# Five chunks instead of three in the last group of mixer 0's output projection, two of seven combinations transposed beside the first FFN pairs

## The chip, the cores and the metric

One core of a Trainium2 chip runs the whole program. The metric is device microseconds of one execution; times of several runs and one profiled execution are given. TensorE (PE) multiplies and transposes, VectorE (DVE), ScalarE (ACT) and GpSimd (POOL) work beside it, and SyncE (SP) issues nearly all transfers. Each engine takes its instructions in a fixed order.

## The reference, cut to what matters

A two-layer decoder trunk on x of 1024 tokens by 1024 channels, float32. Layer 0 has a mixer with two head groups, whose outputs are concatenated (2048 channels) and projected; layer 1 has attention. After each mixer and each FFN comes a LayerNorm of the residual sum:

```python
mix = jnp.concatenate([y_a, y_b], axis=-1) @ w_out
x = layer_norm(ALPHA * x + mix, ln_mix_g, ln_mix_b)
h = causal_dwconv(x @ w_up, conv_w, conv_b)
u, g = jnp.split(h, [D_FF], axis=-1)
x = layer_norm(ALPHA * x + (u * silu(g)) @ w_down, ln_ffn_g, ln_ffn_b)
```

## The kernel before, in words

**Matrix products in float32.** Each operand is split into a rounded high part (a cast on ScalarE, line 116) and a remainder (a subtraction on VectorE, line 117). A product is three matmuls of 128 x 128 by 128 x 512: high by high, high by low, low by high.

**The output projection** (end of `mixer0`, from line 731) runs over 16 chunks of 128 channels in four groups, g = 0 to 3, of 5, 4, 4 and 3 chunks: 0 to 4, 8 to 11, 12 to 15, 5 to 7. Chunks 0 to 7 are y_a, read back from `ya_d`; 8 to 15 are y_b, from `u_d`. `operands` loads a chunk of y and of the weight and splits both into places that the table `places` names: X(n) and E(n) are tiles of two pools, `weights()` and `raws` tiles of the weights' pool, `centre` the two tiles of x.T. For each group `down` takes the 8 token blocks in turn: six matmuls per chunk into one of three PSUM tiles, then `evac` adds the sum to the residual row r[i] on VectorE. In the last group it also runs the LayerNorm and writes r[i] to `x_d`. `late=1` there means that the first three blocks take all chunks but one, and then the last chunk, block by block. The blocks' order is 0, 4, 1, 5, 2, 6, 3, 7.

**The seam.** The FFN's up projection (`ffn_pairs`) multiplies seven combinations of x.T instead of eight quarters: blocks i and i + 4 of r give the corners, halves are added and subtracted on VectorE in `combine` (lines 195 to 209), and each result is transposed by TensorE in runs of four into one of two PSUM banks and split by ScalarE and VectorE (`to_xc`). There are 28 such runs: two for each of blocks 0 to 3, five for each of 4 to 7. They are queued as closures that `down`, and after it `ffn_pairs`, call.

**Pairs.** For j of 0 to 21, pair j holds chunk j of u and of g. `pair_begin` makes two products, x and y, with combinations 0 and 1; `pair_end` makes five, into the banks of x, z and v:

```python
self.multiply(z, w["s1"], 3)
nc.scalar.copy(c[:, 3, :], z)
self.multiply(v, w["s3"], 5)
V.tensor_add(c[:, 3, :], c[:, 3, :], v)
self.multiply(z, w["s4"], 2, more=True)
self.multiply(x, w["s2"], 4, more=True)
nc.scalar.copy(c[:, 1:3, :], x.unsqueeze(1).broadcast_to([P, 2, 512]))
V.tensor_add(c[:, 3, :], c[:, 3, :], x)
self.multiply(v, w["a22"], 6, more=True)
V.tensor_add(c[:, 1:3, :], c[:, 1:3, :], zv.rearrange("p (a b) -> p a b", a=2))
```

GpSimd forms sums of the weights (lines 222 to 225, tile ws) from the loaded chunks (wr); both are split into tiles wo, a ring of ten places. `gate` runs the convolution (ScalarE line 165, four taps on VectorE, line 167), silu and the product u*g. A scheduler orders each engine's instructions when the program is built, so the code's order is only a priority.

Of the kernel before, what the change touches and what calls it, by code (L numbers as in the profile page):

```python
# [10 lines left out]
F32 = mybir.dt.float32  # L11
F32R = mybir.dt.float32r
BF16 = mybir.dt.bfloat16
AF = mybir.ActivationFunctionType
ALU = mybir.AluOpType
# [3 lines left out]
P = 128  # L19
L = 1024  # L20
# [5 lines left out]
NFF = DFF // P  # L26
# [4 lines left out]
XLAG = 2  # L31
# [4 lines left out]
class Ring:  # L36


    def __init__(self, places):
        self.places, self.n = list(places), -1  # L40
# [6 lines left out]
class Net:  # L47
# [11 lines left out]
    def __init__(self, ctx, tc, io):  # L59
        self.ctx, self.tc, self.nc, self.io = ctx, tc, tc.nc, io  # L60
        pool = lambda name, **k: ctx.enter_context(tc.tile_pool(name=name, **k))
        self.const = pool("const", bufs=1)
        self.xp = pool("xT", bufs=1)
        self.wp = pool("w", bufs=1)
        self.ps = pool("ps", bufs=1, space=PSUM)
        self.mm_next, self.after = 0, []
        self.low_engine = self.nc.vector
        self.dr = pool("dr", bufs=1, space=DRAM)
        self.small = pool("small", bufs=4)
        self.consts()  # L70
# [48 lines left out]
    def raw(self, src):  # L119
        t = self.wp.tile([P, D], F32, tag="wraw", name="wraw", bufs=2)  # L120
        self.nc.sync.dma_start(t, src)
        return t
# [69 lines left out]
        h, l = self.xc[m]  # L192
        self.split(h[:, :, ts], l[:, :, ts], ps.rearrange("p (k t) -> p k t", k=4))

    def combine(self, i, r, engine):

        a, b = r[i], r[i + 4]
        lo, hi = slice(0, 512), slice(512, D)
        minus = lambda out, x, y: engine.tensor_tensor(out, x, y, op=ALU.subtract)
        self.to_xc(2, i, b[:, hi])  # L200
        minus(a[:, lo], b[:, lo], a[:, lo])
        self.to_xc(3, i, a[:, lo])
        minus(b[:, lo], b[:, hi], b[:, lo])
        self.to_xc(5, i, b[:, lo])
        minus(a[:, hi], a[:, hi], b[:, hi])
        minus(b[:, hi], b[:, hi], a[:, lo])
        self.to_xc(4, i, b[:, hi])
        engine.tensor_tensor(a[:, hi], a[:, hi], a[:, lo], op=ALU.add)
        self.to_xc(6, i, a[:, hi])

    def pair_a(self, a, ops):

# [46 lines left out]
    def pair_end(self, w, c, x):  # L259
        nc, V = self.nc, self.nc.vector  # L260
        zv = self.mm_ps()
        z, v = zv[:, :512], zv[:, 512:]
        self.multiply(z, w["s1"], 3)
        nc.scalar.copy(c[:, 3, :], z)
        self.multiply(v, w["s3"], 5)
        V.tensor_add(c[:, 3, :], c[:, 3, :], v)  # L266
        self.multiply(z, w["s4"], 2, more=True)
        self.multiply(x, w["s2"], 4, more=True)
        nc.scalar.copy(c[:, 1:3, :], x.unsqueeze(1).broadcast_to([P, 2, 512]))  # L269
        V.tensor_add(c[:, 3, :], c[:, 3, :], x)  # L270
        self.multiply(v, w["a22"], 6, more=True)
        V.tensor_add(c[:, 1:3, :], c[:, 1:3, :], zv.rearrange("p (a b) -> p a b", a=2))  # L272

# [143 lines left out]
    def ffn_pairs(self, layer):  # L417


        nc, tc, io = self.nc, self.tc, self.io  # L420
        V = nc.vector
        y_d = self.dr.tile([NFF, P, L], F32, name="y_d")
        first = [self.rp.tile([P, L], F32, tag=f"r{i}", name="wr") for i in (0, 4, 2)]
        rt = lambda i: self.rp.tile([P, L], F32R, tag=f"r{i}", name="wo")
        ops = Ring([rt(1), rt(5), *self.two(self.eb, 3, "wo", F32R), rt(6), rt(3), rt(7)])
        sums = Ring(self.two(self.eb, 2, "ws"))
        cs = Ring([self.big(self.eb, n, "c").rearrange("p k l -> p (k l)").rearrange("p (a b) -> p a b", a=4)
                   for n in range(2)])
# [2 lines left out]
        raws = Ring(wide["wraw"] + wide["wh"][:1])  # L431
        ug = Ring(wide["wh"][1:] + wide["wl"])

        def raw(c, t=None):
            t = raws() if t is None else t
            nc.sync.dma_start(t, io["ffn_w_up"][layer, c])
            return t
# [7 lines left out]
            V.tensor_mul(u, u, g)  # L445
            nc.sync.dma_start(y_d[j], u)

        a = [raw(j, t) for j, t in enumerate(first[:2])]
        w = [self.pair_a(t, ops) for t in a]
        c = [cs(), cs()]  # L450
        while len(self.after) > 1:
            self.after.pop(0)()
        x = [self.pair_begin(w[0], c[0])]
        self.after.pop(0)()
        then = self.pair_b(w[0], a[0], raw(NFF, first[2]), ops, sums)
        next(then)
        ops.places += [rt(2), rt(0), rt(4)]
        next(then, None)
        x.append(self.pair_begin(w[1], c[1]))
        then = self.pair_b(w[1], a[1], raw(NFF + 1), ops, sums)  # L460
        next(then)
        for j in range(NFF):
            if 2 <= j + 1 < NFF:
                a, b = raw(j + 1), raw(NFF + j + 1)
                w.append(self.pair_a(a, ops))
                then = self.pair_b(w[j + 1], a, b, ops, sums)
# [10 lines left out]
        staged = Ring(staged)  # L477
# [14 lines left out]
        for n, places in enumerate(groups):  # L492
            begins, final = n == 0, n == len(groups) - 1
            ys, ws = [], []
            for place in places():
                for into, src in ((ys, y_d[done]), (ws, io["ffn_w_down"][layer, done])):
                    raw = staged()
# [5 lines left out]
            if begins:  # L503
                staged.places.append(last)
                r = [self.rp.tile([P, D], F32, tag=f"r{i}", name=f"r{i}") for i in range(NT)]
# [21 lines left out]
    def mixer0(self):  # L527
        nc, tc, io = self.nc, self.tc, self.io
        V = nc.vector
# [3 lines left out]
        first = []  # L533
        for k in range(KD):
            if k < 2:
                first.append(self.weight(win[32 + k]))
            raw = self.rp.tile([P, L], F32, tag=f"r{k}", name="xraw")
# [10 lines left out]
        if True:  # L548
            xs = [self.rp.tile([P, D], F32, tag=f"r{c}", name=f"xs{c}") for c in range(NT)]
            if True:  # L550
# [9 lines left out]
                places = [t[:, n * P:(n + 1) * P] for t in rest for n in range(8)]  # L560
# [40 lines left out]
                for j in range(12):  # L601
                    ps = started[j] if j < 2 else self.project(third if j == 2 else win[32 + j])
                    if j < 8:
                        a = cv()
                    else:
                        a = bcs[j - 8]
# [5 lines left out]
                    if j >= 8:  # L612
                        b = btoks[j - 8]
# [108 lines left out]
            r = [self.rp.tile([P, D], F32, tag=f"r{i}", name=f"r{i}") for i in range(NT)]  # L722
# [8 lines left out]
            def operands(chunks, places, stage=self.raw):  # L731
                ys, ws = [], []
                for j, (y, w) in zip(chunks, places, strict=True):
                    h, l = y
                    raw = stage(ya_d[j] if j < 8 else u_d[j - 8])
                    if j < 8:
                        self.split(h, l, raw)
                    else:
                        gcol = self.norm_g[:, j - 8:j - 7]
                        nc.scalar.activation(h, raw, AF.Copy, scale=gcol)  # L740
                        V.scalar_tensor_tensor(out=l, in0=raw, scalar=gcol, in1=h.bitcast(F32),
                                               op0=ALU.mult, op1=ALU.subtract)
                    ys.append((h, l))
                    h, l = w
                    self.split(h, l, stage(io["sc_ssm_w_out"][j]))
                    ws.append((h, l))
                return ys, ws

            def evac(i, ps):
                if g == 0:  # L750
                    V.scalar_tensor_tensor(out=r[i], in0=r[i], scalar=ALPHA, in1=ps, op0=ALU.mult, op1=ALU.add)
                elif g < 3:
                    k = (g - 1) * NT + i
                    V.scalar_tensor_tensor(out=r[i], in0=ps, scalar=rstd[:, k:k + 1], in1=r[i],
                                           op0=ALU.mult, op1=ALU.add)
                else:
                    V.scalar_tensor_tensor(out=r[i], in0=r[i], scalar=1.0, in1=ps, op0=ALU.mult, op1=ALU.add,
                                           accum_out=rsum[:, i:i + 1])
                    self.layer_norm(r[i], ps, rsum[:, i:i + 1], lg, lb, self.spare if i in (3, 6, 7) else None)
                    nc.sync.dma_start(x_d[i * P:(i + 1) * P, :], r[i])  # L760

                    def then():
                        if i < 4:
                            self.to_xc(0, i, r[i][:, :512])
                            self.to_xc(1, i, r[i][:, 512:])
                        else:
                            self.combine(i - 4, r, V)

                    return then

            g = 0
            X, E = [lambda n, pool=pool: of(pool, n) for pool in (self.xe, self.eb)]
            places = [(X(0), X(1)), (X(2), X(3)), (X(4), X(5)), (E(2), E(3)), (weights(), weights())]
            self.down(*operands(range(5), places), evac)
            inv_rms(1, total)
            g = 1
            centre = [self.xp.tile([P, KD, L], F32R, tag=t, name="yw" + t) for t in ("xh", "xl")]
            places = [([t[:, k, :] for t in centre], [t[:, k + 4, :] for t in centre]) for k in range(4)]
            self.down(*operands(range(8, 12), places), evac)
            g = 2  # L780
            places = [(X(0), X(1)), (X(2), X(3)), (X(4), X(5)), (E(2), E(3))]
            self.down(*operands(range(12, 16), places), evac)
            g = 3
            lg, lb = self.two(self.eb, 1, "ln")
            nc.sync.dma_start(lg, io["ln_mix_g"][0].broadcast_to([P, D]))
            nc.sync.dma_start(lb, io["ln_mix_b"][0].broadcast_to([P, D]))
            centre = [self.xp.tile([P, KD, L], F32, tag=t, name="raw" + t) for t in ("xh", "xl")]
            staged = Ring([t[:, k, :] for k in range(3) for t in centre])

            def stage(src):  # L790
                t = staged()
# [1 line left out]
                return t  # L793

            raws = [self.wp.tile([P, D], F32R, tag="wraw", name="yw", bufs=2) for _ in range(2)]
            places = [(E(0), weights()), (weights(), raws), (E(2), E(3))]
            final = operands(range(5, 8), places, stage)
            self.new_combinations()
            self.down(*final, evac, late=1, order=[0, 4, 1, 5, 2, 6, 3, 7], lag=XLAG + 1)
        return r  # L800


# [366 lines left out]
```

## Time and profile before

| | us |
|---|---|
| median of 3 runs | 2845.11 (2842.45 to 2845.29) |
| the profiled execution, its own time | 2843.79 |
| its span, first to last instruction | 2841.8 |
| TensorE busy | 2783.5 |
| VectorE busy | 1629.9 |
| ScalarE busy | 1025.2 |
| GpSimd busy | 336.6 |

Times in rows are microseconds from the span's start. "Busy" is the time an engine has an instruction in it; what stands in brackets behind a row is the idle time before it and the instruction that ended it.

### The profile page before, as it was taken

What the parts mean: (1) busy time and instruction counts of PE and PEld (TensorE: products, weight loads), DVE (VectorE), ACT (ScalarE), POOL (GpSimd) and SP (SyncE); (2) the same over time, 40 slices, a digit from 0 to 9 for tenths busy, and PEclk for the clock granted to TensorE, in tenths of its full rate; (3) what the DMA queues carried; (4) which work ended last, traced back from release to release, by engine and by line L of the source; (5) the groups of instructions that cost most, each with busy time, mean ns of one, the idle gap of its engine ahead of it and who ended that gap; (6) DMA issues with size and microseconds to landing.
All of it is one profiled execution on the core that took longest, in us unless ns stands there. A gap on an engine that the chain in (4) does not pass through costs nothing.

```text
span 2841.8 us, 32602 instructions
## 1 busy us (share of the span) xinstructions
PE 2783.5 (98%) x13162; PEld 2273.1 (80%) x13162; DVE 1629.9 (57%) x2217; ACT 1025.2 (36%) x1502; POOL 336.6 (12%) x264
## 2 busy tenths in 40 slices
PE   8999999999889999999999999999999999999998
PEld 7888888888667777788887888887778888888887
DVE  5445565343777776765465666666565444445446
ACT  5421111321344444442125666666333222222222
POOL 0000000000034333300001222222100000000000
PEclk9999999999899999999999999999999999999999
DMA  3112221352212222263211111112621111111111
GB/s 139 45 67 81 68 82 60 118 204 79 82 60 84 87 75 82 76 214 133 68 74 61 45 53 53 46 60 75 210 80 60 45 46 52 53 58 47 50 42 70
DMA packets 65414, 225.97 MB, mean 80 GB/s; under 512 B 10352, under 2 KB 10736, under 8 KB 65264
## 3 DMA queue, kind: packets, MB, share of 16 engines
q1 hardware_dynamic: 65264, 223.90, 22.9%
q8 instruction: 103, 1.69, 0.2%
q14 instruction: 47, 0.39, 0.0%
HBM read 183.37 MB, written 40.50 MB: 79 GB/s over the span
## 4 chain that ended last, share of the span: by engine, by line
PE 56%; DVE 9%; ACT 3%; issue 1%; DMA 1%; POOL 0%; DVEq 0%; ACTq 0%; POOLq 0%; SPq 0%
PE mm L154 17%; PE mm L290 16%; PE mm L245 7%; PE mm L904 7%; DVE ug L167 3%; PE sm L980 3%; PE mm L940 2%; PE sm L964 2%; DVE wo L117 1%; ACT wo L116 1%; PE mm L1011 1%; DVE c L272 1%; DVE s L945 1%; ACT c L269 1%; DVE r L353 1%
## 5 line engine op out<-in xcount | busy, mean ns | idle before, releaser
L154 PE MATMUL mm<-xh,wh 128*128 128x512 f32 x1408 | 447.7, 395 | 7.7 <-ACT xh L116 7.3
L154 PE MATMUL mm<-xh,wl 128*128 128x512 f32 x1408 | 444.0, 392 | 0.1
L154 PE MATMUL mm<-xl,wh 128*128 128x512 f32 x1408 | 442.3, 392 | 0.0
L117 DVE TENSOR_TENSOR wl<-wraw,wh 128x1024 fp32r<-128x1024 f32 x135 | 165.2, 1224 | 361.9 <-ACT wh L116 361.6
L116 ACT CAST wh<-wraw 128x1024 fp32r<-128x1024 f32 x135 | 141.9, 1051 | 625.9 <-PE mm L154 557.4
L154 PEld LDWEIGHTS mm<-xh,wh 128*128 128x128 f32 x1408 | 263.8, 188 | 66.9 <-ACT xh L116 7.8
L154 PEld LDWEIGHTS mm<-xh,wl 128*128 128x128 f32 x1408 | 264.8, 188 | 58.3 <-issue 2.9
L154 PEld LDWEIGHTS mm<-xl,wh 128*128 128x128 f32 x1408 | 264.8, 188 | 56.8 <-issue 1.7
L290 PE MATMUL mm<-yw 128*128 128x512 f32 x1248 | 292.1, 392 | 1.5 <-ACT mm L349 1.2
L290 PEld LDWEIGHTS mm<-yw 128*128 128x128 f32 x1248 | 233.7, 188 | 50.5 <-ACT mm L349 2.6
L950 POOL TENSOR_TENSOR s<-s,sum 128x128 f32<-128x128 f32 (+7 forms) x128 | 147.6, 1153 | 415.8 <-DVE sum L949 333.1
L245 PE MATMUL mm<-xc,wo 128*128 128x512 f32 x792 | 189.8, 393 | 5.0 <-DVE c L256 5.0
L245 PEld LDWEIGHTS mm<-xc,wo 128*128 128x128 f32 x792 | 147.3, 188 | 43.4 <-DVE c L256 12.2
L904 PE MATMUL mm<-xh,wh 128*128 128x512 f32 x384 | 159.6, 416 | 0.0
L904 PE MATMUL mm<-xh,wl 128*128 128x512 f32 x384 | 157.7, 411 | 0.0
L904 PE MATMUL mm<-xl,wh 128*128 128x512 f32 x384 | 155.5, 405 | 0.0
L352 POOL TENSOR_TENSOR rs<-sq,nhalf 128x1 f32<-128x1 f32 x32 | 18.7, 584 | 991.4 <-DVE sq L351 975.4
L405 DVE SCALAR_TENSOR_TENSOR r<-r,mm 128x1024 f32<-128x1024 f32 x80 | 97.5, 1219 | 66.5 <-PE mm L290 64.6
L245 PE MATMUL mm<-xl,wo 128*128 128x512 f32 x528 | 131.1, 398 | 2.0 <-DVE c L266 2.0
L167 DVE SCALAR_TENSOR_TENSOR ug<-c,ffn_cw,ug 128x1023 f32<-128x1023 f32 (+1 forms) x88 | 125.0, 1461 | 3.2 <-ACT ug L165 3.2
L117 DVE TENSOR_TENSOR p<-sm,p 128x512 fp32r<-128x512 f32 (+1 forms) x192 | 105.2, 553 | 35.5 <-ACT p L116 34.1
L245 PE MATMUL mm<-xh,wo 128*128 128x512 f32 x528 | 124.7, 390 | 0.1
(297 smaller groups left out, 4567.6 us busy)
## 6 DMA issues: line engine op xcount, KB each, us to landing
wraw<-in_sc_ssm_w_in SPq DMA_DIRECT2D x44, 512.0 KB, 3.5
wr<-in_ffn_w_up SPq DMA_DIRECT2D x44, 512.0 KB, 3.4
wraw<-in_ffn_w_up SPq DMA_DIRECT2D x44, 512.0 KB, 3.4
wraw<-in_fox_w_in SPq DMA_DIRECT2D x24, 512.0 KB, 3.4
y_d<-ug SPq DMA_DIRECT2D x22, 512.0 KB, 4.0
raw<-y_d SPq DMA_DIRECT2D x22, 512.0 KB, 4.6
raw<-in_ffn_w_down SPq DMA_DIRECT2D x22, 512.0 KB, 4.3
wraw<-in_ffn_w_down SPq DMA_DIRECT2D x22, 512.0 KB, 3.4
```

The lines of the kernel that those rows point to most:

```text
L116: self.nc.scalar.copy(high, src)
L117: (engine or self.nc.vector).tensor_sub(low, src, high.bitcast(F32))
L154: nc.tensor.matmul(ps[t][:, hs], lhsT=w[:, k * P:(k + 1) * P], rhs=x[:, k, hs], start=(k == 0 and n == 0), stop=(k == KD - 1 and n == 2))
L167: nc.vector.scalar_tensor_tensor(out=out[:, s:], in0=ps[:, :L - s], scalar=w[:, K - 1 - s:K - s], in1=out[:, s:], op0=ALU.mult, op1=ALU.add)
L245: self.nc.tensor.matmul(bank, lhsT=w[a][:, k * P:(k + 1) * P], rhs=x[b][:, k, :], start=not more and (k, n) == steps[0], stop=(k, n) == st ...
L290: nc.tensor.matmul(ps[i][:, hs], lhsT=y[:, i * P:(i + 1) * P], rhs=w[:, hs], start=(j == 0 and m == 0), stop=(j == n - 1 and m == 2))
L405: nc.vector.scalar_tensor_tensor(out=r[i], in0=r[i], scalar=ALPHA if first else 1.0, in1=ps, op0=ALU.mult, op1=ALU.add, **({"accum_out": r ...
L904: nc.tensor.matmul(place, lhsT=a[:, k * P:(k + 1) * P], rhs=x[:, k, half[n]], start=(m == 0), stop=(m == KD * 3 - 1))
L940: nc.tensor.matmul(wide[:, bs], lhsT=q[:, ts], rhs=k[:, bs], start=(m == 0), stop=(m == 1 and bs.stop < n))
L950: nc.gpsimd.tensor_tensor(s[:, :n], s[:, :n], sm.broadcast_to([P, n]), op=ALU.mult)
L964: nc.tensor.transpose(tp[:, c * P:(c + 1) * P], s[:, (b + c) * P:(b + c + 1) * P], self.ident)
L980: nc.tensor.matmul(ops[:, cs], lhsT=v[:, j, e, :], rhs=pt[j // 4 * 2 + m][:, j % 4, cs], start=(j == 0 and m == 0), stop=(j == 2 * g + 1 a ...
```

## The change

The groups have 3, 4, 4 and 5 chunks: 0 to 2, 8 to 11, 12 to 15, 3 to 7. In the last, three chunks are late instead of one, and all five are staged in the tiles of x.T. The places change with that: chunk 3 and 4 of the last group have E(3), E(2) and weight tiles, chunks 5 and 6 X(2) to X(5), which hold combinations 5 and 6 later. Those two are therefore not transposed in `combine` but noted in a list, and `late_combinations` transposes them while the first pairs begin. In `pair_end` the product with s2, its copy and its add come before the product with s3. The FFN's first pairs take other tiles for their weights.

```diff
-    def combine(self, i, r, engine):
+    def combine(self, i, r):
...
-        self.to_xc(5, i, b[:, lo])
...
-        self.to_xc(6, i, a[:, hi])
+        self.late += [(5, i, b[:, lo]), (6, i, a[:, hi])]
+
+    def late_combinations(self):
+        while self.late:
+            self.to_xc(*self.late.pop(0))
...
         self.multiply(z, w["s1"], 3)
         nc.scalar.copy(c[:, 3, :], z)
+        self.multiply(x, w["s2"], 4, more=True)
+        nc.scalar.copy(c[:, 1:3, :], x.unsqueeze(1).broadcast_to([P, 2, 512]))
+        V.tensor_add(c[:, 3, :], c[:, 3, :], x)
         self.multiply(v, w["s3"], 5)
         V.tensor_add(c[:, 3, :], c[:, 3, :], v)
         self.multiply(z, w["s4"], 2, more=True)
-        self.multiply(x, w["s2"], 4, more=True)
-        nc.scalar.copy(c[:, 1:3, :], x.unsqueeze(1).broadcast_to([P, 2, 512]))
-        V.tensor_add(c[:, 3, :], c[:, 3, :], x)
         self.multiply(v, w["a22"], 6, more=True)
...
         x = [self.pair_begin(w[0], c[0])]
+        self.late_combinations()
         self.after.pop(0)()
-        then = self.pair_b(w[0], a[0], raw(NFF, first[2]), ops, sums)
-        next(then)
-        ops.places += [rt(2), rt(0), rt(4)]
-        next(then, None)
+        self.late_combinations()
+        ops.places += [self.rp.tile([P, L], F32R, tag=f"r{i}", name="wo") for i in (0, 4, 1, 5, 2, 6, 3, 7)]
+        for _ in self.pair_b(w[0], a[0], raw(NFF), ops, sums):
+            pass
...
-            places = [(X(0), X(1)), (X(2), X(3)), (X(4), X(5)), (E(2), E(3)), (weights(), weights())]
-            self.down(*operands(range(5), places), evac)
+            places = [(X(0), X(1)), (X(2), X(3)), (X(4), X(5))]
+            self.down(*operands(range(3), places), evac)
...
-            staged = Ring([t[:, k, :] for k in range(3) for t in centre])
+            staged = Ring([t[:, k, :] for k in range(5) for t in centre])
...
-            places = [(E(0), weights()), (weights(), raws), (E(2), E(3))]
-            final = operands(range(5, 8), places, stage)
+            places = [(E(3), raws), (E(2), weights()), (X(2), X(3)), (X(4), X(5)), (E(0), weights())]
+            final = operands(range(3, 8), places, stage)
             self.new_combinations()
-            self.down(*final, evac, late=1, order=[0, 4, 1, 5, 2, 6, 3, 7], lag=XLAG + 1)
+            self.down(*final, evac, late=3, order=[0, 4, 1, 5, 2, 6, 3, 7], lag=XLAG + 1)
```

The scheduled order on TensorE from the last blocks of the third group on, before (mm is a PSUM tile, yw a split operand of the projection, sm a transpose bank, r_3653 to r_3660 the residual's blocks 0 to 7):

```order
L290 MATMUL mm<-yw 128x512 x264
L190 MATMUL sm<-ident,r_3653 128x128 x8
L290 MATMUL mm<-yw 128x512 x20
L190 MATMUL sm<-ident,r_3657 128x128 x4
L290 MATMUL mm<-yw 128x512 x12
L190 MATMUL sm<-ident,r_3653 128x128 x4
L290 MATMUL mm<-yw 128x512 x17
```

and now:

```order
L294 MATMUL mm<-yw 128x512 x312
L190 MATMUL sm<-ident,r_3653 128x128 x8
L294 MATMUL mm<-yw 128x512 x30
L190 MATMUL sm<-ident,r_3657 128x128 x4
L190 MATMUL sm<-ident,r_3653 128x128 x4
L294 MATMUL mm<-yw 128x512 x12
L190 MATMUL sm<-ident,r_3657 128x128 x4
L294 MATMUL mm<-yw 128x512 x18
```

Each row of matmuls before the first transposes and between the next ones is longer: 120 matmuls of the last group stand before the first transposes, where 72 stood, and 30 before the next.

On VectorE, one pair in the steady part of the FFN loop, before, from the add of z and v (L272; L266 is the add of v that s4 waits for, L256 the add of y, L270 the add of x; wo the split weights, ws the sums):

```order
L272 TENSOR_TENSOR c<-c,mm 128x1024
L117 TENSOR_TENSOR wo<-wr,wo 128x1024
L167 SCALAR_TENSOR_TENSOR ug<-c,ffn_cw,ug 128x1023 x2
L167 SCALAR_TENSOR_TENSOR ug<-c,ffn_cw,ug 128x1022
L256 TENSOR_TENSOR c<-c,mm 128x512
L167 SCALAR_TENSOR_TENSOR ug<-c,ffn_cw,ug 128x1022
L117 TENSOR_TENSOR wo<-ws,wo 128x1024
L117 TENSOR_TENSOR wo<-wr,wo 128x512
L445 TENSOR_TENSOR ug<-ug 128x1024
L266 TENSOR_TENSOR c<-c,mm 128x512
L270 TENSOR_TENSOR c<-c,mm 128x512
L117 TENSOR_TENSOR wo<-ws,wo 128x1024
```

and now, from the second instruction of the pair on (L276 stands ahead of it; L260 is the add of y, L271 that of x, L273 that of v):

```order
L117 TENSOR_TENSOR wo<-wr,wo 128x1024
L117 TENSOR_TENSOR wo<-ws,wo 128x1024
L167 SCALAR_TENSOR_TENSOR ug<-c,ffn_cw,ug 128x1023
L260 TENSOR_TENSOR c<-c,mm 128x512
L167 SCALAR_TENSOR_TENSOR ug<-c,ffn_cw,ug 128x1022
L167 SCALAR_TENSOR_TENSOR ug<-c,ffn_cw,ug 128x1023
L117 TENSOR_TENSOR wo<-wr,wo 128x512
L167 SCALAR_TENSOR_TENSOR ug<-c,ffn_cw,ug 128x1022
L117 TENSOR_TENSOR wo<-ws,wo 128x1024
L271 TENSOR_TENSOR c<-c,mm 128x512
L448 TENSOR_TENSOR ug<-ug 128x1024
L273 TENSOR_TENSOR c<-c,mm 128x512
```

The add of x and the second remainder of a sum stood behind the add of v and stand ahead of it now.

On TensorE in the same loop, before (xh and xl hold combinations 0 to 3, xc 4 to 6; a product is 12 matmuls):

```order
L245 MATMUL mm<-xh,wo 128x512 x24
L245 MATMUL mm<-xl,wo 128x512 x12
L245 MATMUL mm<-xc,wo 128x512 x20
L245 MATMUL mm<-xl,wo 128x512 x12
L245 MATMUL mm<-xc,wo 128x512 x16
```

and now:

```order
L249 MATMUL mm<-xh,wo 128x512 x12
L249 MATMUL mm<-xl,wo 128x512 x12
L249 MATMUL mm<-xh,wo 128x512 x2
L249 MATMUL mm<-xc,wo 128x512 x24
L249 MATMUL mm<-xh,wo 128x512 x10
```

Behind these come 12 of s4 (xl) and 12 of a22 (xc). The next pair's x, 12 matmuls, has moved between the products of this pair, and ten of them stand between s3 and s4.

## Rows read from the trace of the kernel before

**Rows 1.** The page's head: span, and busy time of TensorE, its weight loads and the others.
```profile
span 2841.8 us, 32602 instructions
PE 2783.5 (98%) x13162; PEld 2273.1 (80%) x13162; DVE 1629.9 (57%) x2217; ACT 1025.2 (36%) x1502; POOL 336.6 (12%) x264
```

**Rows 2.** Windows: length, busy PE, PEld, DVE, ACT, POOL, granted clock, DMA share, GB/s.
```profile
740.00:760.00 20.00, 18.44 (x91) 14.76 (x90) 19.66 (x34) 8.59 (x15) 2.17 (x4) 0.94 0.40 152
760.00:780.00 20.00, 11.19 (x47) 7.89 (x45) 17.73 (x29) 9.98 (x16) 1.39 (x2) 0.67 0.37 131
...
1016.28:1036.11 19.83, 19.55 (x86) 15.61 (x84) 14.35 (x14) 9.09 (x10) 7.63 (x4) 1.00 0.24 80
```

**Rows 3.** TensorE's timeline over the seam: start, duration, instruction, count, idle time before.
```profile
679.13 60.45 PE L290 MATMUL mm<-yw 128*128 128x512 f32 x264
739.43 1.03 PE L190 MATMUL sm<-ident,r 128*128 128x128 f32 x8
740.22 4.80 PE L290 MATMUL mm<-yw 128*128 128x512 f32 x20
...
810.49 5.47 PE L245 MATMUL mm<-xc,wo 128*128 128x512 f32 x23
817.94 4.57 PE L245 MATMUL mm<-xl,wo 128*128 128x512 f32 x12 [1.98 <-DVE c L266]
...
842.05 5.60 PE L245 MATMUL mm<-xh,wo 128*128 128x512 f32 x24
```

**Rows 4.** VectorE's groups by form, 722.6 to 818 us: count, busy, mean ns, idle before.
```profile
L757 DVE SCALAR_TENSOR_TENSOR r<-r,mm 128x1024 f32<-128x1024 f32 x8 | 9.7, 1212 | 6.0 <-PE mm L290 6.0
...
L117 DVE TENSOR_TENSOR xc<-sm,xc 128x512 fp32r<-128x512 f32 x12 | 8.2, 686 | 2.1 <-ACT xc L116 2.0
L353 DVE SCALAR_TENSOR_TENSOR r<-r,rs,ln 128x1024 f32<-128x1024 f32 x5 | 6.4, 1283 | 0.2
...
L199 DVE TENSOR_TENSOR r<-r 128x512 f32<-128x512 f32 x4 | 2.7, 682 | 0.0
```

**Rows 5.** Timeline of GpSimd and VectorE where a weight sum meets a half combination.
```profile
793.57 1.80 POOL L222 TENSOR_TENSOR ws<-wr 128x512 f32<-128x512 f32 x1 [11.10 <-DMA wr<-in_ffn_w_up]
794.14 1.78 DVE L199 TENSOR_TENSOR r<-r,r 128x512 f32<-128x512 f32 x1
```

**Rows 6.** Timeline of the second group's staging: first and last split, first matmuls.
```profile
595.87 1.15 ACT L740 ACTIVATE ywxh<-wraw,norm_g 128x1024 fp32r<-128x1024 f32 x1 [12.65 <-DMA wraw<-u_d]
...
617.11 1.23 DVE L117 TENSOR_TENSOR ywxl<-wraw,ywxh 128x1024 fp32r<-128x1024 f32 x1 [0.88 <-ACT ywxh L116]
...
635.47 0.72 PE L290 MATMUL mm<-ywxh 128*128 128x512 f32 x2
```

**Rows 7.** Timeline of one pair in the loop, TensorE, VectorE and GpSimd.
```profile
1016.28 5.60 PE L245 MATMUL mm<-xh,wo 128*128 128x512 f32 x24
1017.06 1.21 DVE L272 TENSOR_TENSOR c<-c,mm 128x1024 f32<-128x1024 f32 x1
...
1018.48 2.28 POOL L225 TENSOR_TENSOR ws<-wr,ws 128x512 f32<-128x512 f32 x1
1019.59 4.65 DVE L167 SCALAR_TENSOR_TENSOR ug<-c,ffn_cw,ug 128x1023 f32<-128x1023 f32 x3
...
1021.72 2.88 PE L245 MATMUL mm<-xl,wo 128*128 128x512 f32 x12
...
1024.76 1.27 DVE L167 SCALAR_TENSOR_TENSOR ug<-c,ffn_cw,ug 128x1022 f32<-128x1022 f32 x1
...
1027.24 2.81 POOL L222 TENSOR_TENSOR ws<-wr 128x512 f32<-128x512 f32 x1 [6.48 <-DVE wo L117]
...
1028.89 0.69 DVE L266 TENSOR_TENSOR c<-c,mm 128x512 f32<-128x512 f32 x1
1029.63 3.01 PE L245 MATMUL mm<-xl,wo 128*128 128x512 f32 x12
1030.13 1.29 POOL L223 TENSOR_TENSOR ws<-ws,wr 128x512 f32<-128x512 f32 x1
```

More of the change, by code (lines that the diff above doesn't have):

```diff
@@ L65, in __init__ @@
         self.ps = pool("ps", bufs=1, space=PSUM)
-        self.mm_next, self.after = 0, []
+        self.mm_next, self.after, self.late = 0, [], []
         self.low_engine = self.nc.vector
@@ L193, in to_xc @@
         self.split(h[:, :, ts], l[:, :, ts], ps.rearrange("p (k t) -> p k t", k=4))
-    def combine(self, i, r, engine):
+    def combine(self, i, r):
+        V = self.nc.vector
         a, b = r[i], r[i + 4]
         lo, hi = slice(0, 512), slice(512, D)
-        minus = lambda out, x, y: engine.tensor_tensor(out, x, y, op=ALU.subtract)
         self.to_xc(2, i, b[:, hi])
-        minus(a[:, lo], b[:, lo], a[:, lo])
+        V.tensor_sub(a[:, lo], b[:, lo], a[:, lo])
         self.to_xc(3, i, a[:, lo])
-        minus(b[:, lo], b[:, hi], b[:, lo])
-        self.to_xc(5, i, b[:, lo])
-        minus(a[:, hi], a[:, hi], b[:, hi])
-        minus(b[:, hi], b[:, hi], a[:, lo])
+        V.tensor_sub(b[:, lo], b[:, hi], b[:, lo])
+        V.tensor_sub(a[:, hi], a[:, hi], b[:, hi])
+        V.tensor_sub(b[:, hi], b[:, hi], a[:, lo])
         self.to_xc(4, i, b[:, hi])
-        engine.tensor_tensor(a[:, hi], a[:, hi], a[:, lo], op=ALU.add)
-        self.to_xc(6, i, a[:, hi])
+        V.tensor_add(a[:, hi], a[:, hi], a[:, lo])
+        self.late += [(5, i, b[:, lo]), (6, i, a[:, hi])]
+    def late_combinations(self):
+        while self.late:
+            self.to_xc(*self.late.pop(0))
     def pair_a(self, a, ops):
@@ L422, in ffn_pairs @@
         y_d = self.dr.tile([NFF, P, L], F32, name="y_d")
-        first = [self.rp.tile([P, L], F32, tag=f"r{i}", name="wr") for i in (0, 4, 2)]
-        rt = lambda i: self.rp.tile([P, L], F32R, tag=f"r{i}", name="wo")
-        ops = Ring([rt(1), rt(5), *self.two(self.eb, 3, "wo", F32R), rt(6), rt(3), rt(7)])
+        ops = Ring(self.two(self.eb, 3, "wo", F32R))
+        second = Ring([self.wp.tile([P, L], F32R, tag="wl", name="wo", bufs=2) for _ in range(2)])
         sums = Ring(self.two(self.eb, 2, "ws"))
@@ L446, in gate @@
             nc.sync.dma_start(y_d[j], u)
-        a = [raw(j, t) for j, t in enumerate(first[:2])]
-        w = [self.pair_a(t, ops) for t in a]
+        a = [raw(0), raw(1)]
+        w = [self.pair_a(t, o) for t, o in zip(a, (ops, second))]
         c = [cs(), cs()]
@@ L766, in then @@
                         else:
-                            self.combine(i - 4, r, V)
+                            self.combine(i - 4, r)
                     return then
@@ L780, in mixer0 @@
             g = 2
-            places = [(X(0), X(1)), (X(2), X(3)), (X(4), X(5)), (E(2), E(3))]
+            places = [(X(0), X(1)), (X(2), X(3)), (X(4), X(5)), (E(0), E(1))]
             self.down(*operands(range(12, 16), places), evac)
```

## The prediction

> **What bounds the kernel now.** The first lines of the page say that TensorE does: it is busy for 98% of the 2841.8 us span [rows 1]. A change that keeps the number of matmuls can gain only where TensorE stands, or runs slowly. The windows by stage, read second, show where: until 740 us it is busy all the time, but in 760 to 780 us it has 11.19 of 20 us at a mean granted clock of 0.67 (so partly at the lower level, 1.2 GHz), and in a steady pair of the FFN loop 19.55 of 19.83; in 740 to 760 us VectorE has 19.66 of 20 [rows 2]. So in the seam between mixer 0 and the FFN VectorE sets the pace.
>
> TensorE's timeline, third, sizes the loss. In the loop 24 matmuls take 5.44 us (1016.28 to 1021.72), 0.2267 us each [rows 7]; eight transposes take 0.79 us, 0.40 per run of four [rows 3]. The last group of the output projection begins at 679.13 plus 192 matmuls, at 722.7. From there to 810.49 TensorE does its 144 matmuls, all 28 runs of transposes and 60 matmuls of the first pairs [rows 3]: 204 x 0.2267 + 28 x 0.40 = 57.4 us of work in 87.8 us. Some 30 us are lost here.
>
> **The last group gets five chunks.** The work is the same; two chunks (2 x 8 blocks x 6 = 96 matmuls, 21.8 us) move from the first group into the last, which so begins 21.8 us earlier, at 700.9. I count from that start as 0. A block's evacuation and LayerNorm cost VectorE 1.21 + 1.28 + 1.28 us and small ones, its share of 28 splits and 20 half combinations at 0.68 us about 4 us more [rows 4]: 8 us a block against 4.1 us of matmuls (18) before and 6.8 us (30) now. The first three blocks end 18 matmuls apart, not 6, the first at 12.2 us. VectorE then keeps up until the matmuls end: TensorE needs 240 x 0.2267 = 54.4 us and ten runs of transposes between them, 58.4 us, and what those wait for is ready by then (block 1's combinations at about 53.6 us, where TensorE comes at 53.7).
>
> After that VectorE leads again. From 57.8 us it has, ahead of the split that lets the first pair begin: two weight remainders (2.4), one evacuation (1.2), the two LayerNorm passes of the last block (2.6), six splits (4.1), six half combinations (4.1) and two small ones (0.3), 14.7 us, less 0.07 us of overlap at each of 18 joints: 71.1 us. Here GpSimd forms the sums of pair 0's weights. The row of such a sum beside a half combination shows 1.78 us for 0.68 [rows 5]; I take two collisions (2.2 us) and 0.6 us for the last block's rsqrt, now queued on POOL behind the sums: 74 us. SP has a queue too: the store of the last block stands behind the load of pair 1's second weight, which waits for those sums, and VectorE's next write to that block waits for the store; that is the same 2 us, not more. From 74 us TensorE does 60 matmuls (13.6), eleven runs of transposes (4.4; the eight late combinations lie here) and waits about 2 us for the two transpose banks: 94 us, against 87.8 before. For the next 120 matmuls (810.49 to 842.05, 31.6 us for 27.2, with a wait of 1.98 us in it [rows 3]) I give back 2 us, as the weights of the first pairs are split earlier. Gain of the seam: 21.8 - 6.2 + 2 = 17.6 us. Bounds: no collision and no bank wait, 22; five more collisions, 12.
>
> **The staging.** All groups but the last begin 21.8 us earlier, so their operands must be there. Before, the second group's four chunks were split from 595.87 to 618.34 us, for matmuls at 635.47 [rows 6]. Now the first of them is loaded ahead of the residual's rows, and three stand where four stood: done near 612.5, while the group begins at 613.7 and reaches its fourth chunk 4 us later. Covered by about 5 us; without that cover each us late is a us lost. The other groups have more, and the ten staged loads of the last one start with the third group, 43 us ahead: nothing.
>
> **The order inside a pair.** The product with s2 now comes before that with s3, in all pairs, and this moves the loop. Count from the end of a pair's last product (1016.28 us). Before, VectorE began its add of z, v at 0.78 (1017.06), and ended the add that s4 waits for at 13.30 (1028.89 + 0.69); s4 began at 13.35 and the next end came at 19.83 [rows 7]. So VectorE paces the loop too, though TensorE stands only 0.28 us visibly. Now both remainders of the pair's sums, and the add of x, stand ahead of the gate, where before one remainder and that add came after it. The new chain: add of z, v and one remainder by 2.5 us; then a remainder that must wait until the 12 matmuls of y have read the tile it overwrites (2.7, with 0.2 for the signal 2.9); from there, at starts 0.07 to 0.1 us closer than durations, 1.14 + 1.2 + 0.6 + 2.4 + 0.6 + 1.2 + 1.14 + 0.6 + 1.14 and 0.69 us: 13.6. TensorE arrives there after 60 matmuls, at 13.6: no wait if nothing collides, and 24 matmuls (5.44 us, and 0.1 to restart) later the pair ends at 19.2, 0.6 under today. With GpSimd it is longer: the first filter tap took 2.1 us of its 4.65 us group beside L225 (the rest being two at 1.27), 0.85 too much [rows 7]. On a row like 1027.24, GpSimd waits: 2.81 us for 1.29 while VectorE goes on without a gap [rows 7]. In the new chain GpSimd's first sum waits for a load issued after 2.5 us (about 6 us), so it meets the taps, which follow each other without a gap, and would wait as there; one later sum meets the product u*g. I take half a sum on the chain, 0.6 us, with 0.2 us of restarts: 20.0 us a pair, 0.15 worse, x 19 pairs (22, less the first two and the last): 3 us lost. Bounds: 0.6 better (11 us gained) to 1.2 worse, three sums (23 us lost).
>
> **Sum.** 17.6 - 3 = 14.6 us off the profiled execution, whose own time is 2843.8 (span 2841.8): 2829. The median of the runs shown is 2845.1, 1.3 above, so I predict **2831 us**.
>
> **Rivals.** (1) The loop gains as well: GpSimd always waits and a pair takes 19.4 us. For it, row 1027.24; against it, L167 beside L225. 17.6 + 8 gives 2819. (2) The loop gives back much: a pair takes 20.4, one sum wholly on the chain. 17.6 - 11 gives 2839, at the edge of no change. (3) Slower: GpSimd gets the port between any two VectorE instructions. Its place is between the taps and before u*g; three sums of 1.2 us less the slack make a pair 21.0, and 17.6 - 23 gives 2851. It decides from 20.75 us a pair (19.83 + 17.6/19). For it, rows 5, where sums and combinations alternate; against it, that those combinations depend on each other and leave gaps, which the taps do not. The Trainium skill, on the page SBUF — State Buffer (Who interferes with whom), says that a VectorE instruction with two SBUF inputs and a GpSimd one that reads SBUF lock each other out for the whole instruction, the first to issue winning. Taken by the letter, a sum already waiting would be served when the tap that holds the port ends, which is this rival; row 1027.24 speaks against it, since that sum waited through two VectorE instructions. (4) The change does not do what it says: operands of the second or of the last group come late and TensorE waits there, 10 us of the 17.6 gone: 2841. Against it stand the 5 us of cover.
>
> **How the numbers follow.** Forecast 0.45, rival 1 0.15, rival 2 0.20, rival 3 0.10, rival 4 0.10. Faster or slower begins at 0.2%, 5.7 us, about what a measurement of this kernel tells from no change. The forecast and rival 1 are faster; rival 2 half so; rival 4 mostly not: faster 0.70, same 0.18, slower 0.12. The range from 2817 to 2847 takes in rival 1 below, and above rivals 2 and 4 and the worse bound of the seam; it leaves out most of rival 3.
>
> **What would show it.** In the profile after: the last group's first matmul near 701 us and 24 matmuls of a pair's steady place some 17 us earlier than now; TensorE without a gap until the group's last matmul near 759, then VectorE full and TensorE waiting some 12 us; a pair's period of 20.0 us, with s4 and no longer s2 waiting for VectorE. A period of 20.7 or more, or a gap of TensorE at 614 or 701 us, would prove the forecast wrong; a period near 19.3 would make it too cautious.

## The result: 44 us slower, all of it lost in the FFN loop

| | us |
|---|---|
| before, median of 4 runs | 2843.78 |
| the changed kernel, median of 4 runs | 2888.24 (2886.31 to 2890.77) |
| ratio | 1.0163, 95% interval 1.0151 to 1.0175 |
| predicted | 2831, range 2817 to 2847 |

The page's head of the changed kernel, beside [rows 1]:

```profile
span 2885.9 us, 32653 instructions
...
PE 2793.7 (97%) x13162; PEld 2283.3 (79%) x13162; DVE 1658.5 (57%) x2217; ACT 1025.5 (36%) x1502; POOL 334.1 (12%) x264
```

TensorE and VectorE have as many instructions as before, yet VectorE is busy 28.6 us longer: some of its instructions have become longer. TensorE's timeline over the staging and the seam comes next, beside [rows 3] (start, duration, instruction, count, idle time before it and its releaser):

```profile
612.37 0.72 PE L294 MATMUL mm<-ywxh 128*128 128x512 f32 x2
...
656.03 70.89 PE L294 MATMUL mm<-yw 128*128 128x512 f32 x312
726.76 1.03 PE L190 MATMUL sm<-ident,r 128*128 128x128 f32 x8
...
755.83 4.60 PE L294 MATMUL mm<-yw 128*128 128x512 f32 x19
...
764.65 0.65 PE L190 MATMUL sm<-ident,r 128*128 128x128 f32 x4 [3.35 <-DVE xh L117]
...
772.74 1.94 PE L190 MATMUL sm<-ident,r 128*128 128x128 f32 x8 [5.66 <-DVE r L206]
...
776.00 7.42 PE L249 MATMUL mm<-xh,wo 128*128 128x512 f32 x25
...
799.30 5.85 PE L249 MATMUL mm<-xc,wo 128*128 128x512 f32 x25
...
827.59 2.88 PE L249 MATMUL mm<-xc,wo 128*128 128x512 f32 x12
```

The second group starts at 612.37 without a wait. The last group begins 192 matmuls after 656.03, at 699.6 (forecast 700.9), and ends at 760.4. VectorE then leads, as forecast, and 60 matmuls of the pairs are done at 799.3, where before it was 810.5. So the seam gains 11 us there, and 13 at the pairs' 180th matmul, which ends with the first six of the row 827.59, at 829 (before: 842.05 [rows 3]). The first matmul of the projections of layer 1's attention, further on, tells the rest (one row each of the kernel before and of the changed one):

```profile
1485.95 0.48 PE L904 MATMUL mm<-xh,wh 128*128 128x512 f32 x1
```
```profile
1528.94 0.48 PE L908 MATMUL mm<-xh,wh 128*128 128x512 f32 x1
```

From the 60th matmul to here it took 675.5 us before and 729.6 now: 54 us lost in the loop. One pair of the changed kernel, on TensorE, VectorE and GpSimd, beside [rows 7]:

```profile
893.14 2.88 PE L249 MATMUL mm<-xh,wo 128*128 128x512 f32 x12
...
893.34 1.22 DVE L276 TENSOR_TENSOR c<-c,mm 128x1024 f32<-128x1024 f32 x1 [5.85 <-PE mm L249]
...
895.90 1.22 DVE L117 TENSOR_TENSOR wo<-ws,wo 128x1024 fp32r<-128x1024 f32 x1 [0.21 <-PE mm L249]
...
898.84 3.50 DVE L167 SCALAR_TENSOR_TENSOR ug<-c,ffn_cw,ug 128x1022 f32<-128x1022 f32 x2
...
899.22 2.04 POOL L226 TENSOR_TENSOR ws<-wr 128x512 f32<-128x512 f32 x1 [8.68 <-DMA wr<-in_ffn_w_up]
901.33 2.15 POOL L227 TENSOR_TENSOR ws<-ws,wr 128x512 f32<-128x512 f32 x1
...
902.26 1.78 DVE L117 TENSOR_TENSOR wo<-wr,wo 128x512 fp32r<-128x512 f32 x1
...
906.29 0.68 DVE L271 TENSOR_TENSOR c<-c,mm 128x512 f32<-128x512 f32 x1
906.45 1.27 POOL L228 TENSOR_TENSOR ws<-wr 128x512 f32<-128x512 f32 x1 [2.96 <-DVE wo L117]
906.89 1.92 DVE L448 TENSOR_TENSOR ug<-ug 128x1024 f32<-128x1024 f32 x1
...
907.68 2.25 POOL L229 TENSOR_TENSOR ws<-wr,ws 128x512 f32<-128x512 f32 x1
...
909.46 3.01 PE L249 MATMUL mm<-xl,wo 128*128 128x512 f32 x12 [2.50 <-DVE c L273]
```

The second remainder (895.90) reads the tile of the pair's first two sums and so frees it; it stands ahead of the taps (the multiply-adds of L167). The next sum then starts as soon as its load has landed, at 899.22, in the middle of the taps. Two taps take 3.50 us where one alone takes 1.27, the small remainder 1.78 where it took 0.68, the product u*g 1.92 for 1.21. All of them lie on the chain that the product with s4 (s4 from here on) waits for, and it waits 2.50 us. It is so in every pair. VectorE's groups by form over fifteen pairs, 893.14 to 1239.4 us (count, busy, mean ns, idle before), and TensorE's waits, 880 to 1240 us:

```profile
L167 DVE SCALAR_TENSOR_TENSOR ug<-c,ffn_cw,ug 128x1023 f32<-128x1023 f32 x30 | 53.9, 1796 | 0.0
...
L448 DVE TENSOR_TENSOR ug<-ug 128x1024 f32<-128x1024 f32 x15 | 28.7, 1916 | 0.0
L117 DVE TENSOR_TENSOR wo<-wr,wo 128x512 fp32r<-128x512 f32 x15 | 26.7, 1781 | 0.0
```
```profile
PE mm L249 <- DVE c L273: 37.5, 15, 2.5
```

Against 1.27, 1.21 and 0.68 us this is 2 x 0.52 + 0.70 + 1.10 = 2.85 us a pair. Then something comes on top. Two neighbouring pairs by windows (length, busy PE, PEld, DVE, ACT, POOL, granted clock, DMA share, GB/s), and the s4 of the second:

```profile
893.14:915.03 21.89, 19.39 (x85) 15.62 (x84) 15.86 (x13) 9.19 (x10) 7.68 (x4) 1.00 0.20 73
915.03:938.58 23.55, 21.05 (x85) 16.76 (x84) 15.86 (x13) 9.19 (x10) 7.60 (x4) 0.93 0.20 67
```
```profile
931.35 4.36 PE L249 MATMUL mm<-xl,wo 128*128 128x512 f32 x12 [2.50 <-DVE c L273]
```

The wait is the same 2.50 us, VectorE is as busy, but in the second pair the granted clock is 0.93: the twelve matmuls behind the wait take 4.36 us where they took 3.01, so part of them ran at the lower level (1.2 GHz). Of the fifteen pairs four have a period of 21.9 us and eleven one of 23.5; the mean is 23.08, against 19.81 before.

### The profile page after: what moved, and what is told of

It reads as the page before. It is cut to its first block, busy times and chain, and to the rows that moved or that the text cites. A ratio compares the mean times of both kernels' runs of the same rounds, so it can differ in the third digit from the quotient of the medians.

```text
span 2885.9 us, 32653 instructions
## 1 busy us (share of the span) xinstructions
PE 2793.7 (97%) x13162; PEld 2283.3 (79%) x13162; DVE 1658.5 (57%) x2217; ACT 1025.5 (36%) x1502; POOL 334.1 (12%) x264
## 4 chain that ended last, share of the span: by engine, by line
PE 79%; DVE 13%; issue 4%; ACT 2%; DMA 2%; POOL 1%; SPq 0%; POOLq 0%; DVEq 0%; ACTq 0%
PE mm L154 34%; PE mm L294 20%; PE mm L908 7%; PE mm L249 7%; DVE ug L167 4%; PE sm L984 2%; PE mm L944 2%; PE sm L968 2%; DVE wo L117 2%; PE sm L654 1%; PE mm L1015 1%; DVE r L357 1%; DVE r L354 1%; DVE s L949 1%; DVE p L117 0%
## 5 line engine op out<-in xcount | busy, mean ns | idle before, releaser
L249 PE MATMUL mm<-xl,wo 128*128 128x512 f32 x528 | 148.4, 436 | 42.5 <-DVE c L273 41.7
L249 PEld LDWEIGHTS mm<-xl,wo 128*128 128x128 f32 x528 | 109.1, 210 | 74.8 <-DVE c L273 49.6
L249 PE MATMUL mm<-xh,wo 128*128 128x512 f32 x528 | 132.5, 394 | 1.7 <-DVE c L271 1.7
L167 DVE SCALAR_TENSOR_TENSOR ug<-c,ffn_cw,ug 128x1023 f32<-128x1023 f32 (+1 forms) x88 | 130.6, 1512 | 1.9 <-ACT ug L165 1.7
```

What stands on the lines that cost most here:

```text
L167: nc.vector.scalar_tensor_tensor(out=out[:, s:], in0=ps[:, :L - s], scalar=w[:, K - 1 - s:K - s], in1=out[:, s:], op0=ALU.mult, op1=ALU.add)
L249: self.nc.tensor.matmul(bank, lhsT=w[a][:, k * P:(k + 1) * P], rhs=x[b][:, k, :], start=not more and (k, n) == steps[0], stop=(k, n) == st ...
```

## The experiments

There are seven kernels; each ran beside the kernel before, on the same chip as it. "Period" is the mean time between VectorE's adds of z and v in the steady part. "The port", in the theories, is the way to SBUF that by their account VectorE and GpSimd share.

**The old order inside a pair, the rest of the change kept.**

```diff
-        self.multiply(x, w["s2"], 4, more=True)
...
         self.multiply(v, w["s3"], 5)
         V.tensor_add(c[:, 3, :], c[:, 3, :], v)
         self.multiply(z, w["s4"], 2, more=True)
+        self.multiply(x, w["s2"], 4, more=True)
...
```

The copy and the add behind the product with s2 move with it.

> The change with one part undone: in every pair the product with s3 again comes before that with s2; groups, late combinations and places stay. Theory A (the new order inside a pair loses the time, in the loop): the pair's period falls from the 21.9 to 23.5 us of the changed kernel to 19.8, and the seam's gain is left, 11.2 us at the pairs' 60th matmul (799.3 against 810.5) and 13 at the 180th: 2844 - 13 = 2831 us. Rival B (the late combinations or the new places of the weights cost it): the period stays above 21.5 and the time near 2885.

Measured: 2834.75 us against 2841.74, ratio 0.9974 (0.9965 to 0.9983); period 19.81. Its attention begins here, 10.6 us ahead of the kernel before:

```profile
1475.35 0.48 PE L908 MATMUL mm<-xh,wh 128*128 128x512 f32 x1
```

So theory A: five chunks in the last group and the late combinations gain, and the order inside the pair loses. The seam is worth 10.6 us at this place, and 3 of them are gone again at the end; in the part from the attention on, whose program is the same, the traces of these kernels differ by up to 7 us (1355 to 1362), so that is not a cost of the change that these runs could show.

**The new order alone, in the kernel before.** The edit is the reverse of the one above.

> The kernel before with only the new order inside a pair. Theory A: the loop loses what it lost in the changed kernel (2888 - 2844 + 13 = 57 us), and there is no gain of the seam: 2901 us, period 21.9 to 23.5, s4 waiting 2.5 us for the add of v. Rival B: as before, 2844, period 19.8.

Measured: 2889.48 us, ratio 1.0169 (1.0155 to 1.0182). Theory A in kind, 12 us short in size, and the reason tells the mechanism: its first pairs run at another pace. TensorE's s4 in four pairs, one after the other:

```profile
895.64 3.02 PE L245 MATMUL mm<-xl,wo 128*128 128x512 f32 x12 [0.16 <-DVE c L269]
...
914.95 3.01 PE L245 MATMUL mm<-xl,wo 128*128 128x512 f32 x12 [0.19 <-DVE c L269]
...
934.73 3.06 PE L245 MATMUL mm<-xl,wo 128*128 128x512 f32 x12 [1.78 <-DVE c L269]
...
956.68 3.01 PE L245 MATMUL mm<-xl,wo 128*128 128x512 f32 x12 [2.50 <-DVE c L269]
```

With the same order of the products a pair takes 19.31 us, then 21.9 and more: the first six pairs run at 19.3 to 19.8 us, which is most of the 12 us. VectorE and GpSimd in the second and the third of these pairs:

```profile
904.32 4.87 DVE L167 SCALAR_TENSOR_TENSOR ug<-c,ffn_cw,ug 128x1023 f32<-128x1023 f32 x4
...
909.10 1.22 DVE L117 TENSOR_TENSOR wo<-ws,wo 128x1024 fp32r<-128x1024 f32 x1
...
910.45 2.76 POOL L222 TENSOR_TENSOR ws<-wr 128x512 f32<-128x512 f32 x1 [11.83 <-DVE wo L117]
...
922.99 1.22 DVE L117 TENSOR_TENSOR wo<-ws,wo 128x1024 fp32r<-128x1024 f32 x1
...
924.72 6.94 DVE L167 SCALAR_TENSOR_TENSOR ug<-c,ffn_cw,ug 128x1023 f32<-128x1023 f32 x4
...
926.81 1.55 POOL L222 TENSOR_TENSOR ws<-wr 128x512 f32<-128x512 f32 x1 [8.87 <-DMA wr<-in_ffn_w_up]
```

In the fast pair the sum's remainder stands behind the four taps (4.87 us), and the next sum starts after them. In the slow one it stands ahead, the sum starts among the taps, and they take 6.94 us. The add of z and v begins at 901.42 in the fast pair and at 920.72 in the slow one, so the sum starts 9.0 us behind it, then 6.1.

**The sums cut short, in the changed kernel and in the one before.** They keep their places and what they wait for.

```diff
+        lo, hi = slice(0, 64), slice(512, 576)
         G.tensor_tensor(s12[:, lo], b[:, lo], b[:, hi], op=ALU.add)
...
```

> The changed kernel, with the four GpSimd sums of each pair cut from 512 to 64 columns (the rest of the sums is not formed: left at zero after a fill at the start); the order of VectorE and TensorE in the loop is the same. Theory A1 (the order loses because three sums now hold the port that VectorE needs, 2.7 us a pair, and the wait that follows makes the clock fall, 1.6 us in most pairs): the wait of s4 goes, the period is 19.2 to 19.5, and the time 2888 - 19 x 3.7 = 2818 us. Rival A2 (the chain of VectorE is too long by itself in the new order): the sums take a few tenths less, s4 still waits 2 us, the period stays over 21, the time over 2850.

> The same cut of the sums (64 of 512 columns, the rest left at zero) in the kernel before, as a control. Theory A1: there one tap lost 0.85 us to a sum; without it VectorE's chain is shorter than TensorE's 84 matmuls (19.04 us): period 19.1, the wait of s2 gone, 2844 - 19 x 0.7 = 2831 us. Rival A2: GpSimd plays no part in the loop: 19.83 and 2844.

Measured: 2819.42 us for the changed kernel, ratio 0.9922 (0.9908 to 0.9936), period 19.32; 2831.79 for the kernel before, 0.9961 (0.9945 to 0.9976), period 19.3. Both as theory A1 said. VectorE's work is the same and in the same order; with the short sums the small remainder and the product are back, or nearly, at their length:

```profile
1003.22 1.08 POOL L227 TENSOR_TENSOR ws<-wr 128x64 f32<-128x64 f32 x1 [13.43 <-DMA wr<-in_ffn_w_up]
...
1005.30 0.81 DVE L117 TENSOR_TENSOR wo<-wr,wo 128x512 fp32r<-128x512 f32 x1
...
1009.10 1.22 DVE L452 TENSOR_TENSOR ug<-ug 128x1024 f32<-128x1024 f32 x1
```

So the new chain is not too long by itself; the sums' 2.85 us make it so. They cost the kernel before some 10 us as well (2831.79 against 2841.74).

**The whole sums, held back until the silu of the gate two pairs back.**

```diff
         s12, s34 = sums(), sums()
+        if wait is not None:
+            for s in (s12, s34):
+                G.tensor_copy(s[:, :1], wait[:, L - 1:L])
...
-                then = self.pair_b(w[j + 1], a, b, ops, sums)
+                then = self.pair_b(w[j + 1], a, b, ops, sums, gs[j - 2] if j >= 2 else None)
...
             nc.scalar.activation(g, g, AF.Silu)
+            gs.append(g)
```

> The changed kernel with GpSimd's sums held back: before the sums of a pair GpSimd copies one column of the gate's g, two pairs back, into each half of their tile, so that they begin only when ScalarE's silu of that gate is done; VectorE's and TensorE's order stay. Theory A1 (the sums meet the taps because they start as soon as their load lands): the taps and the remainder behind them are not lengthened (0.94 and 1.10 us of the 2.7 gone), the sums meet only the product u*g; s4 waits 0.5 us, the clock stays up, period 19.8: 2888 - 19 x 3.25 = 2826 us. Rival A3 (whenever the sums run, VectorE loses about as much, as they always take 5 us of the port): s4 still waits 2 us or more, over 2870.

Measured: **2819.28 us against 2844.26, ratio 0.9914 (0.9899 to 0.9929)**; period 19.14. It is faster than both kernels, the changed one by 69 us, with the same order on VectorE and TensorE:

```profile
1000.56 2.88 PE L252 MATMUL mm<-xh,wo 128*128 128x512 f32 x12
...
1006.26 2.47 DVE L167 SCALAR_TENSOR_TENSOR ug<-c,ffn_cw,ug 128x1022 f32<-128x1022 f32 x2
...
1008.65 0.68 DVE L117 TENSOR_TENSOR wo<-wr,wo 128x512 fp32r<-128x512 f32 x1
...
1012.50 1.23 DVE L454 TENSOR_TENSOR ug<-ug 128x1024 f32<-128x1024 f32 x1
1012.52 1.36 POOL L228 COPY ws<-ug 128x1 f32<-128x1 f32 x2 [12.89 <-ACT ug L452]
...
1013.84 1.30 POOL L229 TENSOR_TENSOR ws<-wr 128x512 f32<-128x512 f32 x1
...
1014.37 3.02 PE L252 MATMUL mm<-xl,wo 128*128 128x512 f32 x12
```

Two taps take 2.47 us, the remainder 0.68, the product 1.23, and s4 no longer waits. It did better than expected, since the copies too waited behind u*g (two of them take 1.36 us here, 0.30 in the next kernel, where nothing stands in their way) and the sums so missed the product as well. The price of the new order without collisions is now read directly: from 1000.56, the end of the pair before, to 1014.37 is 13.8 us, as the forecast's 13.6.

**Held back further, until the product u*g.** The column is copied from u behind the product, into a small tile, and from there into the sums' tiles.

> As the last, but the sums wait for the gate's product u*g of two pairs back, the last two-input SBUF work of VectorE before its gap of some 5 us. Theory A1: they run in that gap, no VectorE instruction of the chain is lengthened, s4 does not wait, period 19.2 to 19.4: 2888 - 19 x 3.75 = 2817 us, faster than the kernel before by 25. Rival A3: the sums now come too late for their casts and remainders, or meet other VectorE work: a new wait of over 1 us, period over 20, over 2830.

Measured: 2829.76 us, ratio 0.9950 (0.9933 to 0.9966), period 19.40. No VectorE instruction is lengthened and s4 waits no more, as A1 said, but it is 10 us slower than with the silu. In the loop twelve matmuls of x, and of y, take 2.79 us from start to start where they take 2.72 in the kernel before this one, at a granted clock of 1.00 in both. These two products make 0.15 of the 0.26 us by which a pair is longer; that is 5 us in all, and the other 6 lie behind the loop, in the part whose program is the same. What makes the matmuls slower is open, and nothing was tried for it.

**The new order of the products, with the remainder behind the taps.** Two idle matmuls move VectorE's schedule.

```diff
         V.tensor_add(c[:, 3, :], c[:, 3, :], v)
+        fill = self.sm_ps()
+        for k in range(2):
+            nc.tensor.matmul(fill, lhsT=w["a22"][0][:, :P], rhs=self.xc[6][0][:, k % 4, :], start=True, stop=True,
+                             skip_group_check=True)
         self.multiply(z, w["s4"], 2, more=True)
```

> The changed kernel, with two matmuls more in each pair, behind s3, into a transpose bank that nobody reads; their only purpose is that the scheduler then puts the remainder of the first sum behind the taps, where the changed kernel has it ahead of them; the products keep the new order, s2 before s3. TensorE's own work grows to 86 x 0.2267 = 19.5 us a pair. Theory A1 (the sums meet the taps because their tile is freed ahead of the taps): the sums now start behind the taps, s4 waits 0.5 us at most, period 19.5 to 19.9, 2888 - 19 x 3.35 = 2824 us, faster than the changed kernel by 64 with more work. Rival A4 (the new order of the products costs its 3 us a pair wherever the remainder stands): period over 21.5, over 2865.

Measured: 2838.41 us, ratio 0.9988 (0.9978 to 0.9997), period 19.94. The kernel is 50 us faster than the changed one with more work for TensorE:

```profile
1000.56 1.22 DVE L117 TENSOR_TENSOR wo<-ws,wo 128x1024 fp32r<-128x1024 f32 x1
...
1001.91 2.76 POOL L226 TENSOR_TENSOR ws<-wr 128x512 f32<-128x512 f32 x1 [12.45 <-ACT ug L451]
...
1006.41 3.01 PE L249 MATMUL mm<-xl,wo 128*128 128x512 f32 x12
```

The remainder stands behind the taps, the sum starts behind it (its row names the silu, which ended within 0.02 us of the remainder), and TensorE stands less than 0.2 us ahead of s4. The period is just above what A1 said. The total is 14 us over: the sum took the gain for 19 pairs, but the pairs ahead of 893 us gained next to nothing (an add of z and v at 892.8 here, at 893.34 in the changed kernel), and the period is 0.2 us above the 19.73 of the sum. Rival A4 falls.

## Why the prediction was wrong

**The seam: right in kind, mis-sized.** The early start (699.6), no gap at the second group, VectorE's lead after the group's end (760.4, forecast 759) and the pairs' first matmul at 776.0 (forecast 774.9) came as forecast. The gain was put at 17.6 us with bounds of 12 and 22; with the old order inside a pair, 10.6 of it is left at the attention. The term at fault is the way from the pairs' first matmul to the 60th: 20 us were given, it took 23.3, so that the gain there is 11.2 where 15.6 were forecast. The 2 us given back in the next 120 matmuls came (11.2 us at the 60th, 13 at the 180th; with the old order inside a pair 9.4 and 11). Two collisions had been forecast ahead of the pairs' first matmul, and two of about 1 us came there (two weight remainders at 759.42 took 3.43 us for 2.4, a LayerNorm pass at 765.77 took 2.30 for 1.28). On the way to the 60th there were more, and the forecast had none: a half combination of 1.48 us at 793.09, a small remainder of 1.42 at 798.02, each 0.68 or 0.69 alone. With the sums cut short the early pairs ran 4 us ahead (an add of z and v at 844.2, against 848.4 with the sums held back, which leaves the seam as it is); short sums are also done sooner, so these 4 us are not the price of collisions alone.

**The order inside a pair: the chain right, its collisions wrong.** The chain of 13.6 us without GpSimd was right (13.8). The step that failed is "it meets the taps [...] and would wait as there; one later sum meets the product u*g. I take half a sum on the chain, 0.6 us". The sum did not wait: it came between two taps, the next sum between a tap and the small remainder, a third ahead of the product, 2.85 us in every pair, where half a sum (0.6 us) had been put. The forecast had drawn "GpSimd waits" from one row, 1027.24 [rows 7], and the same group held the row that spoke against it (a tap of 2.1 us).

**That is rival 3, which had a chance of 0.10, and its price was wrong.** It put a pair at 21.0 us, from three sums of 1.2 less the slack; the pairs at full clock take 21.9. But the forecast's own chain has no slack: TensorE arrives when VectorE ends, at 13.6 us. Three sums of 1.2 us on it make 19.2 + 3.6 = 22.8 us a pair, 2.97 more than before, and 2845.1 - 17.6 + 19 x 2.97 = 2884 us, not 2851. The bound of 1.2 us worse a pair, also called three sums, has the same fault.

The Trainium skill, on the page SBUF — State Buffer (SBUF: two separate sides, and Who interferes with whom), has the rule that the forecast set aside: of a GpSimd instruction that reads SBUF and a VectorE instruction with two SBUF inputs, the one that starts first holds the shared port pair for the whole instruction. The loop of the changed kernel agrees with it: the taps, the small remainder and the product grew by 1.04, 1.10 and 0.70 us. The rows 1027.24 [rows 7] and 1001.91 do not: there a sum began to wait in one VectorE instruction, and the next one went first. The Trainium skill says on the same page (Who interferes with whom) that a VectorE instruction with at most one SBUF input, outside its two-port modes, does not contend with GpSimd. The trace agrees: the add of x, with one operand in PSUM, took 0.68 us beside the sum at 906.45, which took 1.27.

**The clock was in no case.** Behind the wait that the collisions open TensorE's clock fell in 11 of 15 pairs, 1.6 us each. The forecast put nothing for it, though its own rows had the sign: behind a wait of 1.98 us the twelve matmuls at 817.94 took 4.57 us [rows 3]. Against the kernel with the sums held back (19.14), a pair's 23.08 us are 2.75 from the collisions and 1.6 x 11/15 = 1.2 from the clock; about a third of the loop's loss was not on the list. That the wait is its cause is shown as far as the kernels without it keep 1.00 in the loop; a wait of 2.50 us without a fall stands in four pairs, and what decides between them is open.

**The staging** cost nothing, as forecast; rival 4 did not come.

## What to carry to other kernels

Where GpSimd and VectorE both read SBUF, ask what frees the tile that GpSimd writes: moving one VectorE remainder ahead of a run of two-input instructions let the sums start some 3 us earlier in the pair (5.9 us behind the add of z and v in the changed kernel, against 9.0 in the fast pairs of the new order alone) and meet the run. If such a sum is needed late, hold it back to VectorE's gap; a copy of one column did that here and was worth 2.4% of the changed kernel's time, 0.9% of the time before. When a bound is priced, put every collision on the chain in full, unless a row shows slack there. And price a new wait of TensorE of some 2 us with the clock that may fall behind it.

## What was not expected of the hardware

- GpSimd gets the port between VectorE instructions that follow without a gap, but not always. A sum that began to wait in a tap, 0.9 to 1.0 us ahead of its end, came next (899.22, 901.33). One that began in a small remainder, 0.47 us ahead of its end, let the product go first and took 2.76 us (1001.91 with two idle matmuls; 1027.24 in [rows 7] alike, 0.53 us ahead). What decides between the two is open.
- The same wait of 2.50 us is followed by twelve matmuls in 3.01 to 3.04 us or in 4.22 to 4.62.
